# A decoder block on one core: GLU by row blocks, convolution in wide sums, merge products with tokens on the partition

## The chip, the cores and the metric

The kernel runs on one core of a Trainium2 chip. The metric is the device time of the execution in microseconds (us). Its engines are named as in the profile: PE is TensorE (matmul), PEld its weight load, DVE VectorE, ACT ScalarE, POOL GpSimd, SP SyncE, on whose queue nearly all loads are issued. Each engine works through its own instructions in the order in which the program has them.

## The reference, cut to what matters

One decoder layer over 256 tokens and 2048 channels, all in float32:

```
h    = rmsnorm(x) * (1 + sc1) + sh1          # sh1, sc1, g1, ... = silu(c) @ w_ada + b_ada
proj = h @ w_in                              # q, six k/v parts, gates, GLU input (a, g), merge gates (ga, gb)
o    = sparse attention of 16 heads
u    = causal_dwconv(a * sigmoid(g), 31 taps)
y_b  = silu(layernorm(u)) @ conv_pw_w + conv_pw_b
y_a  = o @ w_o_nsa
merged = sigmoid(ga) * y_a + sigmoid(gb) * y_b
x = x + g1 * (merged @ w_out)
x = x + g2 * conv_ffn(rmsnorm(x) * (1 + sc2) + sh2);  return rmsnorm(x)
```

The weights are some 400 MB in all, and each is read once.

## The kernel before, in words

**Products.** A weight tile of 128 x 1024 floats is loaded (`raw`, four buffers), then split: ScalarE rounds it to `hi` (L213), VectorE makes `lo = raw - hi` (L214), three buffers each; in the middle part every fourth tile takes a buffer of its own from the pool `more`. An activation is split in the same way. A product is the sum of three matmuls, hi x hi, hi x lo, lo x hi. `prod_w` (L240) holds the weights still and streams 256 tokens: its result has channels on the partition, and one row block (128 rows) of 512 columns is 12 matmuls of 256 columns (L248, L250, L251). `prod_x` (L227) holds the tokens still and streams the weights: its result has tokens on the partition, and the same row block is 6 matmuls of 512 columns (L235 to L237).

**Order.** The main line of products is emitted in program order. Beside it stand three queues: `heads_q` (attention), `conv_q` (convolution, LayerNorm) and `ada_q` (products with w_ada). After each weight tile `tick` (L117) pops those items whose engines, by the planner's account `load`, are not ahead of TensorE's. The account adds a cost per tile (L207 to L224) and one per item; an engine may lag TensorE by 8000 ns at most. `drain` empties a queue. The weight splits and the heads have high priority in the ordering of instructions on each engine.

**First stage.** w_ada's columns for sh1 and sc1 (33.5 MB) are multiplied on TensorE by groups of two column blocks (`ada_group`, L370, L379), turned into columns (L386), and give two blocks of the normed input h1 each. Beside them, for each of h1's 16 row blocks as it becomes ready, the GLU's first seven column blocks of both halves are summed in PSUM (`glu_first`, L402, L409 to L411). The other nine blocks follow as full products of 384 columns.

**Convolution.** Two blocks at a time, 30 taps of each as one multiply-add on VectorE (L457), first tap and last copy on ScalarE. Its order is that of `conv_q`, from the end of the first stage on.

**Attention.** Head by head, scores two heads ahead of values (`AHEAD`), paced by the planner's account; the products for q, the first three `ga` gates and attention share one stretch.

**Merge.** Four chunks each of ga, `w_o_nsa`, gb, `conv_pw_w`, all by `prod_w`; `merged` has channels on the partition, which is what `w_out` (by `prod_x`) needs as its stationary side. The bias of conv_pw is a column per block. Steps of ada for g1, sh2 and sc2, 96 in all, each a load of 512 KB and a multiply-add of 1024 columns on VectorE (L280), are paced by `PACE` until attention is over and by 1500 after the w_o_nsa products.

Of the kernel before, what the change touches and what calls it, by code (L numbers as in the profile page):

```python
# [16 lines left out]
P = 128  # L17
D = 2048
# [33 lines left out]
DF = 1.0  # L52
WEND = 25
TL = 1
HP = 300
AHEAD = 2
SB = 8
PACE = 5000
# [3 lines left out]
def block_kernel(ctx, tc, x, c, w_ada, b_ada, norm1_g, w_in, cmp_pe, w_kc1, w_kc2, w_vc1, w_vc2,  # L62
# [44 lines left out]
    queues = [deque(), deque(), deque()]  # L107
    heads_q, conv_q, ada_q = queues
    load = {"pe": 0.0, "dve": 0.0, "act": 0.0, "dma": 0.0}

    los = deque(maxlen=LAG)

# [4 lines left out]
    def tick():  # L117
        for e in ("dve", "act", "dma"):
            load[e] = max(load[e], load["pe"] / DF - 8000.0)
        go = True  # L120
        while go:
            go = False
            for q in queues:
                if q and all(load[e] * DF <= load["pe"] for e in q[0][0]):
                    cost, f = q.popleft()
                    use(**cost)
                    with ExitStack() as es:
                        es.enter_context(tc.issue_after(los[0]))
                        if q is heads_q and HP:
                            es.enter_context(tc.high_priority(HP))  # L130
                        f()
                    go = True

# [67 lines left out]
    ext, turn = [None], [0]  # L201

    def wtile(src, k0, nk, c0, w):
        raw = wp.tile([P, WT], F32, tag="raw", name=nm("raw"), bufs=4)
        turn[0] += 1
        pool, bufs = (ext[0], 1) if ext[0] is not None and turn[0] % 4 == 0 else (wp, 3)
        hi = pool.tile([P, WT], F32R, tag="hi", name=nm("hi"), bufs=bufs)  # L207
        lo = pool.tile([P, WT], F32R, tag="lo", name=nm("lo"), bufs=bufs)
# [9 lines left out]
    def tiles(src, nk, c0, w):  # L218
        step = WT // w
        for k0 in range(0, nk, step):  # L220
            m = min(step, nk - k0)
# [3 lines left out]
            use(pe=m * w * 2.53)  # L225
            tick()
# [13 lines left out]
    def prod_w(act, src, c0, w, nk=KB):  # L240

        nb = w // P
        acc = ps_acc.tile([P, 4, T], F32, tag="acc", name=nm("accw"))
        for k, hi, lo in tiles(src, nk, c0, w):
            for b in range(nb):
                s = slice(b * P, (b + 1) * P)
                last = k == nk - 1 and (b % 2 == 1 or b == nb - 1)
                nc.tensor.matmul(acc[:, b, :], hi[:, s], act[:, k, 0, :], start=k == 0 and b % 2 == 0, stop=False,  # L248
                                 skip_group_check=True)
                nc.tensor.matmul(acc[:, b, :], hi[:, s], act[:, k, 1, :], start=False, stop=False, skip_group_check=True)  # L250
                nc.tensor.matmul(acc[:, b, :], lo[:, s], act[:, k, 0, :], start=False, stop=last, skip_group_check=True)  # L251
        return acc[:, :nb, :]
# [90 lines left out]
    par_first()  # L343
    ss = st(NT * 2)
    for t in range(NT):
        for j in range(2):
            scr = t4([P, WT])
            nc.scalar.activation(scr, xt[:, t, j * WT:(j + 1) * WT], AF.Square, accum_out=ss[:, 2 * t + j:2 * t + j + 1])
    s2 = st(NT)
    nc.vector.reduce_sum(s2, ss.rearrange("p (t n) -> p t n", n=2), axis=AX.X)  # L350
    r = rsqrt_cols(s2, NT, 1.0 / D)
    xh = bigt([P, NT, D])
    for t in range(NT):
        nc.vector.tensor_scalar(xh[:, t, :], xt[:, t, :], r[:, t:t + 1], None, op0=ALU.mult)
    xhT = bigt([P, KB, T])
    for k in range(0, KB, 2):
        p_ = pt([P, 2, T])
        for j in range(2):
            for t in range(NT):
                nc.tensor.transpose(p_[:, j, t * P:(t + 1) * P], xh[:, t, (k + j) * P:(k + j + 1) * P], ident)  # L360
        nc.scalar.copy(xhT[:, k:k + 2, :], p_)

    h1 = actt()
    NA = 7
    u = bigt([P, KB, T])
    ada_v = w_ada[:, :2 * D].rearrange("(k p) (s c) -> p k s c", p=P, s=2)

    def ada_group(j):  # L370

        p_ = pt([P, 2, T])
        for n in range(8):
            side, k = n // 4, n % 4 * 4
            own = n % 3 == 2
            raw = (wp if own else first).tile([P, 4, T], F32, tag="araw", name=nm("araw"), bufs=2 if own else 4)
            nc.sync.dma_start(raw, ada_v[:, k:k + 4, side, j * T:(j + 1) * T])
            for i in range(4):
                nc.tensor.matmul(p_[32 * i:32 * i + 32, side, :], cz[:, k + i, :], raw[:, i, :], start=k == 0,  # L379
                                 stop=k == KB - 4, skip_group_check=True)  # L380
            yield
        acc = t4([P, 2, T])
        nc.scalar.copy(acc, p_)
        p_ = pt([P, 4])
        for i in range(4):
            nc.tensor.matmul(p_[:, i:i + 1], acc[:, i // 2, (i % 2) * P:(i % 2 + 1) * P], ones[:, 0:1], start=True, stop=True)  # L386
# [4 lines left out]
        yield  # L391

    acc_g = ps_acc.tile([P, 4, T], F32, tag="acc", name="acc_g")
    acc_a = ps_acc.tile([P, 4, T], F32, tag="acc", name="acc_a")
    acc_x = [pt([P, 2, T]) for _ in range(3)]

    def first_out(which, b):
        if b < 4:
            return (acc_g, acc_a)[which][:, b, :], b % 2
        if b < 6:  # L400
            return acc_x[which][:, b - 4, :], b - 4
        return acc_x[2][:, which, :], which  # L402
# [10 lines left out]
    with tc.tile_pool(name="first", bufs=4) as first:  # L413
# [13 lines left out]
        for _ in stream:  # L427
            pass
# [575 lines left out]
```

## Time and profile before

| | |
|---|---|
| median of 3 runs | 1765.85 us (1764.63 to 1767.06) |
| profiled execution, its own time | 1765.94 us |
| its span, first to last instruction | 1764.2 us |
| mean granted TensorE clock | 0.986 of full speed |
| read from memory | 402.8 MB, 230 GB/s over the span |

Busy times and shares are of the span. A matmul's busy time includes its way through the pipeline, so matmuls overlap: the rate of a stage is read from how far apart they start, or from their count in a window. The stages by the last instruction that reads a product: GLU to 282 us, k, v and the first half of q to 415, attention with the rest of q and three ga gates to 600, w_o_nsa and the last gate to 717, gb to 813, conv_pw to 912, w_out to 1003, then the feed-forward part, which the change does not touch.

### The profile page before, as it was taken

The numbers are of one execution on the slowest core, as the hardware profiler recorded it, in microseconds if no ns is written. First come the engines' busy times: TensorE is split into PE (matmuls) and PEld (weight loads), VectorE is DVE, ScalarE is ACT, GpSimd is POOL, SyncE is SP. The second block draws the span as 40 slices with busy tenths as digits, with TensorE's granted clock in tenths as the row PEclk, the third lists the DMA queues.
The fourth block names the chain that finished last, engine by engine and source line by source line (L and its number), as shares of the span: only waits on it lengthen the run. The fifth ranks groups of instructions, "written<-read, shape, count | busy, mean of one in ns | idle before, by whom it ended". The sixth has DMA issues, their size and how long they took to land.

```text
span 1764.2 us, 29690 instructions
## 1 busy us (share of the span) xinstructions
PE 1712.7 (97%) x11844; PEld 1551.8 (88%) x11844; DVE 1286.4 (73%) x1852; ACT 872.9 (49%) x1223; POOL 5.5 (0%) x22
## 2 busy tenths in 40 slices
PE   5999999999999999999999899999999999999997
PEld 3777999899999999999988888888888888888886
DVE  2233999998999898877886677776467776586665
ACT  4333444344768634563344465554455554345553
POOL 0000000000000000000000000000000000000000
PEclk8999999999999999999999999999999999999999
DMA  9996777884764676789887667676666767656663
GB/s 305 352 345 225 228 225 231 266 286 143 235 198 130 203 241 214 250 300 317 292 306 259 199 202 226 215 224 222 219 213 212 220 213 219 212 183 189 188 192 127
DMA packets 270198, 406.83 MB, mean 231 GB/s; under 512 B 12876, under 2 KB 181612, under 8 KB 269420
## 3 DMA queue, kind: packets, MB, share of 16 engines
q1 hardware_dynamic: 268652, 400.49, 71.4%
q10 hardware_dynamic: 1408, 4.46, 0.7%
q8 instruction: 92, 1.51, 0.4%
q14 instruction: 46, 0.38, 0.1%
HBM read 402.80 MB, written 2.10 MB: 230 GB/s over the span
## 4 chain that ended last, share of the span: by engine, by line
PE 93%; DMA 3%; DVE 2%; ACT 1%; issue 1%; SPq 0%; DVEq 0%; ACTq 0%
PE accp L261 18%; PE accw L251 11%; PE accw L248 11%; PE accw L250 11%; PE accp L262 9%; PE accx L236 6%; PE accx L237 6%; PE accx L235 6%; DMA araw<-in_w_ada_dram 2%; PE pt L379 1%; PE pt L675 1%; DVE lo L214 1%; PE pt L714 1%; PE pt L409 1%; PE pt L410 1%; PE pt L411 1%
## 5 line engine op out<-in xcount | busy, mean ns | idle before, releaser
L213 ACT CAST hi<-raw 128x1024 fp32r<-128x1024 f32 (+2 forms) x562 | 575.1, 1024 | 765.9 <-PE accw L250 273.3
L214 DVE TENSOR_TENSOR lo<-raw,hi 128x1024 fp32r<-128x1024 f32 (+2 forms) x562 | 668.6, 1191 | 375.4 <-ACT hi L213 363.8
L261 PE MATMUL accp<-act,hi 128*128 128x512 f32 x1408 | 492.4, 395 | 0.0
L251 PE MATMUL accw<-act,lo 128*128 128x256 f32 x1696 | 484.1, 286 | 2.0 <-DVE lo L214 2.0
L250 PE MATMUL accw<-act,hi 128*128 128x256 f32 x1696 | 483.8, 285 | 0.0
L248 PE MATMUL accw<-act,hi 128*128 128x256 f32 x1696 | 483.8, 285 | 0.0
L262 PE MATMUL accp<-act,lo 128*128 128x256 f32 x1408 | 393.6, 280 | 0.0
L251 PEld LDWEIGHTS accw<-act,lo 128*128 128x128 f32 x1696 | 325.5, 192 | 5.0 <-DVE lo L214 3.0
L248 PEld LDWEIGHTS accw<-act,hi 128*128 128x128 f32 x1696 | 325.8, 192 | 3.2 <-issue 2.4
L250 PEld LDWEIGHTS accw<-act,hi 128*128 128x128 f32 x1696 | 325.7, 192 | 2.4 <-issue 2.2
L261 PEld LDWEIGHTS accp<-act,hi 128*128 128x128 f32 x1408 | 264.1, 188 | 62.1 <-issue 0.2
L262 PEld LDWEIGHTS accp<-act,lo 128*128 128x128 f32 x1408 | 265.6, 189 | 0.3 <-issue 0.2
L236 PE MATMUL accx<-lo,act 128*128 128x512 f32 (+2 forms) x664 | 227.6, 343 | 1.3 <-DVE lo L214 1.3
L235 PE MATMUL accx<-hi,act 128*128 128x512 f32 (+2 forms) x664 | 227.2, 342 | 0.0
L237 PE MATMUL accx<-hi,act 128*128 128x512 f32 (+2 forms) x664 | 226.8, 342 | 0.0
L457 DVE SCALAR_TENSOR_TENSOR cacc<-big,cw,cacc 128x255 f32<-128x255 f32 (+24 forms) x480 | 201.3, 464 | 0.3
L280 DVE SCALAR_TENSOR_TENSOR t<-araw,cs,t 128x1024 f32<-128x1024 f32 x120 | 153.6, 1280 | 25.3 <-DMA araw<-in_w_ada_dram 25.2
L236 PEld LDWEIGHTS accx<-lo,act 128*128 128x128 f32 x664 | 125.8, 189 | 18.4 <-DVE lo L214 2.6
L235 PEld LDWEIGHTS accx<-hi,act 128*128 128x128 f32 x664 | 125.8, 189 | 14.5 <-ACT hi L213 0.2
L237 PEld LDWEIGHTS accx<-hi,act 128*128 128x128 f32 x664 | 125.8, 189 | 14.3 <-issue 0.4
L918 DVE SCALAR_TENSOR_TENSOR t<-t,fw,t 128x254 f32<-128x254 f32 (+1 forms) x176 | 73.5, 478 | 0.0
L916 ACT ACTIVATE t<-t,fw 128x256 f32<-128x256 f32 x88 | 48.0, 593 | 1.3 <-DVE t L913 1.3
(214 smaller groups left out, 1198.7 us busy)
## 6 DMA issues: line engine op xcount, KB each, us to landing
araw<-in_w_ada_dram SPq DMA_DIRECT2D x192, 512.0 KB, 5.4
raw<-in_ffn_w_up_dram SPq DMA_DIRECT2D x176, 512.0 KB, 4.5
raw<-in_w_in_dram SPq DMA_DIRECT2D x116, 512.0 KB, 4.6
raw<-in_ffn_w_down_dram SPq DMA_DIRECT2D x88, 512.0 KB, 4.7
raw<-in_w_in_dram SPq DMA_DIRECT2D x48, 384.0 KB, 3.9
raw<-in_w_o_nsa_dram SPq DMA_DIRECT2D x32, 512.0 KB, 4.7
raw<-in_conv_pw_w_dram SPq DMA_DIRECT2D x32, 512.0 KB, 5.5
raw<-in_w_out_dram SPq DMA_DIRECT2D x32, 512.0 KB, 4.7
```

The source lines that it names most:

```text
L213: nc.scalar.copy(hi[:, :n], raw[:, :n])
L214: los.append(nc.vector.tensor_tensor(lo[:, :n], raw[:, :n], hi[:, :n], op=ALU.subtract).ins)
L235: nc.tensor.matmul(o, act[:, k, 0, s], hi, start=k == 0, stop=False)
L236: nc.tensor.matmul(o, act[:, k, 0, s], lo, start=False, stop=False)
L237: nc.tensor.matmul(o, act[:, k, 1, s], hi, start=False, stop=k == nk - 1)
L248: nc.tensor.matmul(acc[:, b, :], hi[:, s], act[:, k, 0, :], start=k == 0 and b % 2 == 0, stop=False, skip_group_check=True)
L250: nc.tensor.matmul(acc[:, b, :], hi[:, s], act[:, k, 1, :], start=False, stop=False, skip_group_check=True)
L251: nc.tensor.matmul(acc[:, b, :], lo[:, s], act[:, k, 0, :], start=False, stop=last, skip_group_check=True)
L261: nc.tensor.matmul(acc[:, b], hi[:, s], act[:, k], start=k == 0, stop=False, skip_group_check=True)
L262: nc.tensor.matmul(acc[:, b, 0, :], lo[:, s], act[:, k, 0, :], start=False, stop=k == KB - 1, skip_group_check=True)
L280: nc.vector.scalar_tensor_tensor(acc, raw, cs[:, k:k + 1], acc, op0=ALU.mult, op1=ALU.add)
L457: nc.vector.scalar_tensor_tensor(acc[:, s:], u[:, b, :T - s], cw[:, CW - 1 - s, b:b + 1], acc[:, s:], op0=ALU.mult, op1=ALU.add)
```

## The change

- **GLU.** The 16 row blocks are worked in four quarters. For each quarter all eight chunks of 512 columns are summed over four row blocks and added into `u` and `gl` in SBUF (`glu_out`); sigmoid and product follow in the last quarter. The ada columns that a quarter of h1 needs are loaded beside the quarter before: sh1 on TensorE (`ada_pe`), sc1 on VectorE (`ada_dve`); the first two pairs (`ada_lead`) wholly on TensorE. Three quarters stand in the first stage; the last is the start of the middle part.
- **Convolution.** Three blocks at a time (six groups, the last of one block). 18 of 30 taps are a product per block on ScalarE and one sum over the group on VectorE, 12 stay as they were. One accumulator tile and one product tile. The pool `more` is gone.
- **Attention.** `AHEAD` 1; `deal(n)` spreads the queued steps evenly over the next n weight tiles.
- **Merge.** ga, w_o_nsa, gb and conv_pw by `prod_x`; `merged` has tokens on the partition and is turned for `w_out` by 32 transposes, three and four tiles behind each chunk; the bias is loaded as rows.
- **Planner.** Other costs (2.75 for 2.53 a column, 150 for 60 of VectorE a tile), `PACE` 6500; the 32 steps for g1 are queued when the taps are done, at 1500, the others get 1500 after the gb products.

```diff
+    def deal(n):
+        share[:] = len(heads_q) / n, 0.0
...
+        share[1] += share[0]
+        while heads_q and share[1] >= 1.0:
+            share[1] -= 1.0
+            give(heads_q)
...
-        pool, bufs = (ext[0], 1) if ext[0] is not None and turn[0] % 4 == 0 else (wp, 3)
...
-        use(dma=1.43 * n, act=190 + n / 1.2, dve=60 + n / 0.96)
+        use(dma=1.43 * n, act=190 + n / 1.2, dve=150 + n / 0.96)
...
+    def glu_out(q, n, acc):
+        s = slice(4 * (n // 2), 4 * (n // 2) + 4)
+        dst = (gl, u)[n % 2]
+        if q == 0:
+            nc.scalar.copy(dst[:, s, :], acc)
+            return
+        nc.vector.tensor_add(dst[:, s, :], dst[:, s, :], acc)
...
+        def ada_dve(box, q, side):
+            for k in range(0, KB, 2):
+                raw = ada_raw([P, 2, QW])
+                nc.sync.dma_start(raw, ada_v[:, k:k + 2, side, q * QW:(q + 1) * QW])
...
+            stream = ada_quarter(q + 1)
+            for n in range(8):
...
+                    acc = acc_w()
+                    sum_w(acc, h1, w_in, glu_c0(n), q * KQ, KQ, True, True)
+                glu_out(q, n, acc)
+                for _ in range(3):
+                    next(stream, None)
...
+    WIDE = tuple(s for s in range(2, CW) if s % 5 not in (0, 2)) + (1,)
...
+                nc.scalar.mul(box["p"][:, b - b0, s:], u[:, b, :T - s], cw[:, CW - 1 - s, b:b + 1])
...
+                    nc.vector.tensor_add(acc[:, :, s:], acc[:, :, s:], prod[:, :, s:])
...
+        for s in WIDE:
+            conv_q.extend(({"act": 500}, product(b, s)) for b in blk)
+            conv_q.extend(narrow.popleft() for _ in range(min(n, len(narrow))))
+            conv_q.append(({"dve": 170 + n * 265}, wide(s)))
...
-        yp = prod_w(oT, w_o_nsa, n * 512, 512)
+        yp = prod_x(oT, w_o_nsa, n * 512, 512)
...
+        yp = prod_x(uT, conv_pw_w, n * 512, 512)
+        y = t4([P, NT, 512])
+        for t in range(NT):
+            nc.vector.tensor_add(y[:, t, :], yp[:, t, :], bias)
+            nc.vector.tensor_mul(y[:, t, :], y[:, t, :], gbs[:, t, s])
+            nc.vector.tensor_add(merged[:, t, s], merged[:, t, s], y[:, t, :])
+        coming.extend([3 + i, turn_m(4 * n + 2 * i)] for i in range(2))
```

## Rows read from the trace of the kernel before

**Rows 1.** The page, part 1: busy us, share of the span, instructions.

```profile
PE 1712.7 (97%) x11844; PEld 1551.8 (88%) x11844; DVE 1286.4 (73%) x1852; ACT 872.9 (49%) x1223; POOL 5.5 (0%) x22
```

**Rows 2.** The page, part 4: the chain that ended last, by engine.

```profile
PE 93%; DMA 3%; DVE 2%; ACT 1%; issue 1%; SPq 0%; DVEq 0%; ACTq 0%
```

**Rows 3.** Windows: length, busy us (count) of each engine, clock, DMA share, GB/s.

```profile
34.00:178.00 144.00, 133.01 (x1183) 106.99 (x1180) 42.18 (x62) 47.40 (x63) 1.06 (x2) 0.93 0.92 303
178.00:282.00 104.00, 104.00 (x867) 103.84 (x866) 97.82 (x164) 46.67 (x61) 0.00 (x0) 1.00 0.80 230
282.00:415.00 133.00, 133.00 (x1128) 124.73 (x1127) 122.56 (x227) 57.15 (x69) 1.27 (x3) 1.00 0.81 255
415.00:625.00 210.00, 210.00 (x1564) 198.70 (x1563) 189.81 (x397) 139.33 (x315) 0.52 (x1) 0.98 0.59 181
836.00:912.00 76.00, 74.87 (x602) 72.83 (x601) 64.25 (x72) 28.80 (x31) 0.00 (x0) 1.00 0.87 297
912.00:1004.00 92.00, 89.30 (x489) 76.99 (x487) 60.49 (x69) 41.23 (x53) 0.00 (x0) 1.00 0.74 241
...
420.00:440.00 20.00, 20.00 (x125) 18.35 (x126) 15.10 (x43) 7.33 (x20) 0.00 (x0) 0.86 0.26 79
180.00:700.00 520.00, 520.00 (x4163) 500.27 (x4163) 477.00 (x884) 273.02 (x473) 1.79 (x4) 0.99 0.71 218
```

**Rows 4.** Timeline of PE, start and length: eleven and thirteen matmuls, first and last.

```profile
640.00 0.28 PE L251 MATMUL accw<-act,lo 128*128 128x256 f32 x1
...
641.20 0.28 PE L248 MATMUL accw<-act,hi 128*128 128x256 f32 x1
...
1500.07 0.39 PE L237 MATMUL accx<-hi,act 128*128 128x512 f32 x1
...
1502.79 0.39 PE L237 MATMUL accx<-hi,act 128*128 128x512 f32 x1
```

**Rows 5.** Timeline of PE: the first GLU matmul, the first behind the stage.

```profile
34.15 0.58 PE L409 MATMUL acc_g<-act,hi 128*128 128x256 f32 x1
...
177.92 0.28 PE L248 MATMUL accw<-act,hi 128*128 128x256 f32 x1
```

**Rows 6.** Windows of PE and PEld alone, lines 379, 386 and 155 in turn.

```profile
34.00:178.00 144.00, 32.85 (x444) 11.14 (x440) 0.93 0.92 303
...
34.00:178.00 144.00, 7.21 (x56) 6.79 (x56) 0.93 0.92 303
...
34.00:178.00 144.00, 2.79 (x10) 1.43 (x10) 0.93 0.92 303
```

**Rows 7.** Windows, as rows 3, of two stretches in which loads are dense.

```profile
60.00:140.00 80.00, 75.34 (x711) 60.30 (x710) 24.83 (x35) 26.94 (x35) 0.00 (x0) 0.98 1.04 343
780.00:800.00 20.00, 20.00 (x169) 20.00 (x169) 15.12 (x13) 8.26 (x8) 0.00 (x0) 1.00 0.97 345
```

**Rows 8.** Groups by line and shape: count, busy us, mean ns, idle before.

```profile
L214 DVE TENSOR_TENSOR lo<-raw,hi 128x1024 fp32r<-128x1024 f32 x476 | 581.9, 1223 | 286.0 <-ACT hi L213 283.0 <-PE accw L251 0.6
L684 DVE SCALAR_TENSOR_TENSOR s<-dist,pt 128x512 f32<-128x512 f32 x16 | 10.9, 683 | 0.1
...
L704 ACT ACTIVATE s<-s,st 128x256 f32<-128x256 f32 x32 | 14.3, 497 | 0.0
```

**Rows 9.** The chain in order of time: start, us, four transposes between products.

```profile
1014.07 0.44 PE pt L901 x4
```

**Rows 10.** Windows of VectorE alone, line 457 (the taps).

```profile
180.00:690.00 510.00, 201.33 (x480) 0.99 0.71 218
```

**Rows 11.** Timeline of ACT: the last gb gate is read.

```profile
813.37 1.02 ACT L840 ACTIVATE big<-accw 128x1024 f32<-128x1024 f32 x1
```

**Rows 12.** Windows of VectorE alone, line 280 (ada steps).

```profile
836.00:912.00 76.00, 23.78 (x20) 1.00 0.87 297
```

**Rows 13.** Waits: us in total, times, longest us.

```profile
DVE lo L214 <- ACT hi L213: 363.8, 315, 7.2
...
PEld accw L251 <- DVE lo L214: 3.0, 5, 1.1
```

More of the change, by code (lines that the diff above doesn't have):

```diff
@@ L122, in tick, with give @@
             go = False
[L123 to L131, printed above, removed]
-                    go = True
+            for q in (conv_q, ada_q):
+                if q and all(load[e] <= load["pe"] for e in q[0][0]):
+                    give(q)
+                    go = True
+    def give(q):
+        cost, f = q.popleft()
+        use(**cost)
+        with ExitStack() as es:
+            es.enter_context(tc.issue_after(los[0]))
+            if q is heads_q:
+                es.enter_context(tc.high_priority(HP))
+            f()
     def drain(q):
@@ L416, in block_kernel, with ada_raw @@
         nc.vector.tensor_copy(cz[:, :, 0], cs)
[L418 to L428 removed]
+        seen = [0]
+        def ada_raw(shape):
+            seen[0] += 1
+            own = seen[0] % 3 == 0
+            return (wp if own else first).tile(shape, F32, tag="araw", name=nm("araw"), bufs=2 if own else 4)
@@ new lines, in ada_quarter @@
+        def ada_quarter(q):
+            box = {}
+            js = range(q * KQ // 2, (q + 1) * KQ // 2)
+            turns = [ada_dve(box, q, 1), (x for j in js for x in ada_pe(box, j, 0))]
+            for _ in range(8):
+                for g in turns:
+                    next(g)
+                    yield
+            for g in turns:
+                for _ in g:
+                    pass
+            for n, j in enumerate(js):
+                modulate(j, halves(box[0, j]) + halves(box[1][:, n * T:(n + 1) * T]))
+                yield
@@ new lines, in ada_lead @@
+        def ada_lead(j):
+            box = {}
+            for side in range(2):
+                yield from ada_pe(box, j, side)
+            modulate(j, halves(box[0, j]) + halves(box[1, j]))
+            yield
+        par_first()
+        lead = ada_lead(0)
+        for _ in range(4):
+            next(lead)
+        ss = st(NT * 2)
+        for t in range(NT):
+            for j in range(2):
+                scr = t4([P, WT])
+                nc.scalar.activation(scr, xt[:, t, j * WT:(j + 1) * WT], AF.Square,
+                                     accum_out=ss[:, 2 * t + j:2 * t + j + 1])
@@ L486, in block_kernel @@
+    for n in range(8):
+        acc = acc_w()
+        sum_w(acc, h1, w_in, glu_c0(n), (NQ - 1) * KQ, KQ, True, True)
+        glu_out(NQ - 1, n, acc)
+        there = 2 * n + 2 if n % 2 else 0
+        while done + 3 <= there:
+            conv_blocks(done, 3)
+            done += 3
+    conv_blocks(done, KB - done)
     kcv = sgt([P, 4, T])
```

316 lines of the change are left out of this document (170 added, 146 removed).

## Prediction

> **What bounds the kernel now.** I read the busy shares first: TensorE is busy 97% of the span, VectorE 73%, ScalarE 49% [rows 1]. The chain of waits agrees: 93% of what ended last is TensorE's own work [rows 2]. A busy TensorE is not yet one at its best rate, so I then took the windows by stage and counted matmuls. In the stages from 178 us on it issues without a break: 867 instructions in 104 us, 1128 in 133 us [rows 3]. The timeline gives the rate: ten 256-column weight products take from 640.00 to 641.20 us, 0.120 us each; twelve of 512 columns from 1500.07 to 1502.79 us, 0.2267 us each [rows 4]. Only two places leave time on the table: the first stage (busy counts 133 of 144 us, but with a clock of 0.93 and, below, only 122 us of work) and the merge products with the ada loads beside them (602 instructions in 76 us, where 0.120 us would give 633) [rows 3]. VectorE is nearly full from 178 to 625 us (97.8 of 104, 122.6 of 133, 189.8 of 210 us), so it is the engine that can take a gain back; ScalarE has room in all stages [rows 3].
>
> **Term 1, GLU by row blocks.** The first product starts at 34.15 us and the first stage ends at 177.92 us [rows 5]: 143.8 us. In it TensorE does 672 GLU matmuls (7 column blocks x 2 x 3 x 16) at 0.120 = 80.6 us, ada matmuls 32.9 us, column turns of ada 7.2 us, parameter transposes 2.8 us [rows 6]; sum 123.5, so 20 us are lost there. Then the other 9 blocks, 864 matmuls at 0.120 = 103.7 us, end the GLU at 281.6 us. After the change three quarters of the GLU run beside the loads: 1152 matmuls = 138.2 us. Half of the ada columns go from TensorE to VectorE, which leaves 320 of 512 ada instructions, some 256 of them after 34 us, at 32.85/444 each = 18.9 us; turns and transposes stay at 10. Sum 167 us, ending at 201 us without a gap; the last quarter adds 384 x 0.120 = 46.1, to 247 us. What could hold it: the transfers (w_ada 33.5 MB, three quarters of the GLU weights 25.2 MB, x 2.1 MB: 61 MB at the 343 GB/s of the loaded stretch [rows 7] are 178 us, less than 201), and VectorE (48 splits at 1.22 = 59, 48 ada sums of 512 columns by the nearest row, 0.68, = 33, 16 sums of GLU blocks at 1.22 = 20, some 10 more [rows 8]: 122 of 167 us; it had 42 of 144 [rows 3]). So TensorE becomes the bound of this stage, but three engines at 75 to 100% with queues in order won't run without gaps: I take 10 us lost, half of today's, end at 257 us, gain 25 us. Ends: 34 (no gap), 13 (today's 20 us stay).
>
> **Term 2, merge products.** Sixteen products of 512 columns and 16 row blocks change from weights-stationary to tokens-stationary. A row block costs 12 x 0.120 = 1.440 us now and 6 x 0.2267 = 1.360 us after [rows 4]; 256 row blocks x 0.080 = 20.5 us gained, all on the path. Added: merged must be turned back, 32 transposes at 0.44/4 = 0.11 us [rows 9], 3.5 us. Net 17.
>
> By the Trainium skill (TensorE: Matmul & The Clock Gate, Back-to-back issue gap) an isolated matmul is followed after N/2.4 + 2.5 ns, 109 ns for 256 columns and 216 for 512. By that rule the swap would gain only 4 us instead of 20.5; the trace does not agree for 256 columns (120 ns [rows 4]).
>
> **Term 3, the convolution.** 480 taps cost 201.3 us of VectorE [rows 10], 0.419 each. 288 of them become a ScalarE product and a wide sum: 120.7 us leave VectorE; 90 sums of three blocks (about 720 columns, between 0.68 for 512 and 1.22 for 1024 [rows 8]: 0.90) and 18 of one (0.42) add 88.6. VectorE gains 32 us; ScalarE gets 288 x 0.49 (the scaled 256-column ACTIVATE, 497 ns [rows 8]) = 141 us. None of this is on the path by itself. But the conv starts after the last GLU quarter's second pair (about 217 us, now 180) and has a shorter span to finish in, so VectorE stays as full as it was. All 480 taps are done by 690 us now [rows 10] and conv_pw starts when the last gate has been read at 813 us [rows 11], so some 50 us of delay are covered. I put this at 0; ends -4 (VectorE is relieved) and +6.
>
> **Term 4, attention.** 415 to 625 us holds six products (138 us) and 72 us of attention; ScalarE is busy 139 us, VectorE 190 us of 210 [rows 3]. About a third of the new ScalarE products falls here (38 sums, 114 products x 0.49 = 56 us), so ScalarE goes to some 195 of 205 us with exponentials and transposed copies in TensorE's chain. Spreading the heads evenly and looking one head ahead instead of two evens the peaks but lets a head's chain show. I take +4 us; ends -6 (the clock dip to 0.86 from 420 to 440 us goes [rows 3]) and +20.
>
> **Term 5, ada beside the merge products.** The planner gives ada loads less before conv is done (pace 6500 for 5000) and puts them behind it. A tile of a product allows 2816 - 1464 = 1352 ns of other transfers, so 0.9 of a step of 1500; VectorE's account allows (2816 - 1217 - 700)/1130 = 0.8, plus what is unspent. In the four conv_pw products that is some 30 steps instead of the 20 of 836 to 912 us [rows 12]. VectorE then needs 32 x 1.22 + 30 x 1.28 + merges of 5.5 us each (six 512-column operations of 0.68, two splits of 0.69) = 99 us in 91; the transfers are 62 x 0.524 MB = 32.5 MB, 94 us at 345 GB/s [rows 7]. The stage already loses 4 us at 20 steps, and waits for lo are what it loses them to [rows 13]. I take +8; ends 0 (the backlog slides into the w_out products, where VectorE has 60 of 92 us [rows 3]) and +13. No further ada work is left at the end of w_out, so the drain behind it costs nothing. The sum merged needs 4.1 us of VectorE behind the last conv_pw product; its transposes are held back three and four tiles (8 and 11 us), which covers it, unless VectorE is behind by more than 4 us; that is within the +13. The bias rows travel on ScalarE's queue, four of 256 KB, hidden.
>
> **Sum.** -25 - 20.5 + 3.5 + 0 + 4 + 8 = -30 us. The profiled execution took 1765.9 us (span 1764.2 and 1.7 around it), the median of the runs is 1765.85, so both give **1736 us**.
>
> **Rivals.**
> 1. Everything hides: the first stage runs without gaps (-34), ada slides into w_out (0), attention gains 4: 1765.9 - 34 - 17 - 4 = 1711 us. For it: VectorE loses 32 us of taps, and 60 of 92 us in w_out. Against: the 4 us already lost at 20 steps.
> 2. Little is left: the gaps of the first stage stay (-13), the merge stage costs its full 13, attention 8: 1765.9 - 13 - 17 + 13 + 8 = 1757 us. For it: three nearly full engines in order.
> 3. Slower: the wide sum waits for ScalarE. There is one product tile, so each sum frees it, three products follow, and the next sum stands on VectorE in front of later weight splits. ScalarE's queue holds its weight copies, which wait for TensorE (lo waited for hi 363.8 us in 315 waits, 1.15 us each [rows 13]). If VectorE is blocked 0.8 us at each of 108 sums, that is 86 us; it has about 43 free in this part (520 us from 180 to 700 less 477 busy [rows 3]; after the change the span is shorter by some 45 us, and its work, by the taps and the GLU splits done earlier, by as much), so 43 come through: 1779 us. It decides from (43 + 30)/108 = 0.68 us a sum. Against: the twelve plain taps of each block stand between the products, 0.42 us each, and three buffers of hi and lo give TensorE 5.8 us of lead.
> 4. The page's spacing: term 2 gains 4 less 3.5, the rest as forecast: 1753 us.
>
> **Chances.** Forecast 0.52 (its own range 1724 to 1748), rival 1 0.20, rival 2 0.14, rival 3 0.11, rival 4 0.03. A change of 0.2% (3.5 us) is what a measurement of this kernel can tell. Faster: 0.52 + 0.20 + 0.03 and 0.09 of rival 2 = 0.84; the same 0.05, the upper end of rival 2; slower 0.11, rival 3. Eight in ten lie from 1708 to 1764: rival 1 with 3 us of room, and rival 2 with a stall of 7 us more; left out is rival 3.
>
> **What would show it.** The GLU's last matmul near 257 us, and a granted clock nearer 1 than 0.93 in the first stage; 90 matmuls of 512 columns in 20 us in all merge products; stalls behind lo in conv_pw of 8 us; ScalarE above 90% in attention. The forecast is wrong if the GLU ends after 270 us, or if VectorE sits idle before the wide sums for over half a microsecond each.

## The result, and the profile after: slower by 0.7%

The changed kernel takes 1778.57 us (median of 4, 1777.32 to 1779.70) against 1765.24 us for the kernel before: ratio 1.0071, 95% interval 1.0051 to 1.0091. The forecast was 1736 us. Busy shares and the chain of waits of the kernel after, which answer to [rows 1, 2]:

```profile
PE 1690.7 (95%) x10148; PEld 1467.6 (83%) x10148; DVE 1322.6 (74%) x1732; ACT 982.3 (55%) x1489; POOL 6.1 (0%) x28
...
PE 83%; DVE 6%; DMA 5%; ACT 4%; issue 2%; DVEq 0%; SPq 0%; ACTq 0%
```

TensorE has 22 us less to do, as intended, but a tenth of the chain has gone from it to VectorE, ScalarE and the loads. The place is found by following the same events through both kernels. In the timeline of the kernel after (start, length, line): the compressed keys are read, the third ga gate, the last exponential of the last head, the first and the second w_o product, the reciprocals of the LayerNorm's variance, the last gb gate, the second w_out product.

```profile
285.29 1.01 ACT L595 COPY sg<-accw 128x1024 f32<-128x1024 f32 x1
540.07 1.00 ACT L839 COPY sg<-accx 128x1024 f32<-128x1024 f32 x1
615.88 0.19 ACT L796 ACTIVATION_READ_ACCUMULATOR s<-s,st 128x1 f32 x1
633.88 1.22 DVE L947 TENSOR_TENSOR big<-accx,sg 128x1024 f32<-128x1024 f32 x1
642.84 1.22 DVE L947 TENSOR_TENSOR big<-accx,sg 128x1024 f32<-128x1024 f32 x1
771.77 1.75 DVE L907 RECIPROCAL t<-t 128x256 f32<-128x256 f32 x1
804.60 1.02 ACT L953 ACTIVATE big<-accx 128x1024 f32<-128x1024 f32 x1
969.44 1.28 DVE L1004 TENSOR_TENSOR t<-accx,gb 128x512 f32<-128x512 f32 x2
```

The same events in the kernel before (the last gb gate is [rows 11]):

```profile
305.87 1.01 ACT L488 COPY sg<-accw 128x1024 f32<-128x1024 f32 x1
596.46 1.02 ACT L731 COPY sg<-accw 128x1024 f32<-128x1024 f32 x1
594.37 0.19 ACT L688 ACTIVATION_READ_ACCUMULATOR s<-s,st 128x1 f32 x1
624.98 1.22 DVE L831 TENSOR_TENSOR big<-accw,sg 128x1024 f32<-128x1024 f32 x1
648.33 1.22 DVE L831 TENSOR_TENSOR big<-accw,sg 128x1024 f32<-128x1024 f32 x1
732.62 1.75 DVE L791 RECIPROCAL t<-t 128x256 f32<-128x256 f32 x1
957.89 1.29 DVE L874 TENSOR_TENSOR t<-accx,gb 128x512 f32<-128x512 f32 x2 [0.41 <-PE accx L237]
```

The differences give the account. An event marks TensorE's progress only where TensorE hasn't run ahead of it. When the first w_o product of the kernel after is read, some 59 of the second one's 96 matmuls are done (37 are left, from 634 to 643 us), and when its last conv_pw product is read, at 931 us, 60 of w_out's are done, so these two events are no ends of a stretch here; the second w_o product and the second w_out product are. The forecast column splits the terms of the prediction over the same stretches (a merge product at 16 x 0.080 = 1.28 us; five lie in the second stretch, seven in the third, four in the fourth).

| stretch | forecast | measured |
|---|---|---|
| start to the compressed keys | -25 | -20.6 |
| to the second w_o product | -6.4 + 4 = -2.4 | +15.1 |
| to the last gb gate | -9.0 | -3.3 |
| to the second w_out product | -5.1 + 3.5 + 8 = +6.4 | +20.3 |
| to the end of the span | 0 | 0.0 |
| span of the profiled execution | -30 | +11.5 |

So the first stage's gain came, and two stretches gave it back and more: of the 41.5 us between forecast and result, 17.5 lie in the second stretch and 13.9 in the fourth, 5.7 in the third and 4.4 in the first. Windows of the kernel after (length, busy us and count of PE, PEld, DVE, ACT, POOL, clock, DMA share, GB/s), to be read against [rows 3]: the first stage, the stretch between third gate and first w_o product, and conv_pw.

```profile
34.00:201.00 167.00, 159.68 (x1374) 144.50 (x1366) 106.75 (x132) 64.80 (x77) 0.00 (x0) 0.96 0.94 312
...
540.00:634.00 94.00, 78.22 (x372) 60.52 (x371) 74.26 (x152) 73.59 (x194) 0.63 (x2) 0.95 0.33 110
...
805.00:931.00 126.00, 111.61 (x483) 90.23 (x484) 103.59 (x102) 43.54 (x45) 0.00 (x0) 0.93 0.91 322
```

From 540 to 634 us TensorE runs the w_o products head by head as the heads come (156 of the 372 instructions); the others are mostly the heads' small ones. It is idle for 15.8 of the 94 us, and the loads fall to 110 GB/s. The kernel before has no wait of TensorE from 415 to 650 us. The waits of TensorE and the loads' hold on VectorE from 400 to 1020 us (total, times, longest) name the rest:

```profile
DVE t L299 <- DMA araw<-in_w_ada_dram: 21.2, 23, 2.5
...
PE pt L312 <- DVE t L299: 11.4, 1, 11.4
...
PE accx L248 <- DVE lo L226: 10.5, 8, 5.0
...
PE pt L764 <- DVE t L758: 8.0, 1, 8.0
...
PE pt L817 <- ACT s L812: 5.4, 2, 4.5
```

L764 and L817 are in the attention; 7.9 of the 10.5 us of waits for lo come by 812 us, behind the LayerNorm's work on VectorE; L312 turns an ada column at 917 us and waits for the sums of ada steps (L299), which wait for their tiles. VectorE's timeline shows what the wait at L764 was for. L748 and L758 are steps of a softmax of the attention, L548 and L567 the taps and wide sums of the convolution:

```profile
556.14 1.23 DVE L226 TENSOR_TENSOR lo<-raw,hi 128x1024 fp32r<-128x1024 f32 x1
557.28 1.19 DVE L548 SCALAR_TENSOR_TENSOR cacc<-big,cw,cacc 128x229 f32<-128x229 f32 x3
559.01 0.40 DVE L748 TENSOR_REDUCE st<-t 128x16 f32<-128x240 f32 x1 [0.55 <-ACT t L742]
559.33 0.89 DVE L567 TENSOR_TENSOR cacc<-cacc,cprod 128x711 f32<-128x711 f32 x1
...
561.71 0.89 DVE L567 TENSOR_TENSOR cacc<-cacc,cprod 128x705 f32<-128x705 f32 x1
562.52 0.41 DVE L758 TENSOR_TENSOR t<-t,st 128x240 f32<-128x240 f32 x1
```

From 554.6 to 563.0 us, while TensorE waits, taps and sums take some 5 us of VectorE.

### The profile page after: what moved, and what is told of

It is laid out like the page before. It is cut to its first block, busy times and chain, and to the rows that moved or that the text cites. A ratio compares the mean times of both kernels' runs of the same rounds, so it can differ in the third digit from the quotient of the medians.

```text
span 1775.7 us, 26510 instructions
## 1 busy us (share of the span) xinstructions
PE 1690.7 (95%) x10148; PEld 1467.6 (83%) x10148; DVE 1322.6 (74%) x1732; ACT 982.3 (55%) x1489; POOL 6.1 (0%) x28
## 4 chain that ended last, share of the span: by engine, by line
PE 83%; DVE 6%; DMA 5%; ACT 4%; issue 2%; DVEq 0%; SPq 0%; ACTq 0%
PE accp L280 18%; PE accx L248 11%; PE accx L249 10%; PE accx L247 10%; PE accp L281 9%; PE accw L259 6%; PE accw L262 6%; PE accw L261 6%; DMA araw<-in_w_ada_dram 4%; DVE t L299 2%; DVE lo L226 2%; PE pt L420 1%; ACT cprod L558 1%; ACT hi L225 1%; ACT s L796 1%
## 5 line engine op out<-in xcount | busy, mean ns | idle before, releaser
L225 ACT CAST hi<-raw 128x1024 fp32r<-128x1024 f32 x546 | 572.4, 1049 | 684.0 <-PE accx L249 287.7
L226 DVE TENSOR_TENSOR lo<-raw,hi 128x1024 fp32r<-128x1024 f32 x546 | 665.3, 1220 | 315.8 <-ACT hi L225 313.9
L280 PE MATMUL accp<-act,hi 128*128 128x512 f32 x1408 | 492.3, 395 | 0.0
L248 PE MATMUL accx<-lo,act 128*128 128x512 f32 (+2 forms) x1176 | 433.3, 369 | 10.9 <-DVE lo L226 10.5
L247 PE MATMUL accx<-hi,act 128*128 128x512 f32 (+2 forms) x1176 | 430.6, 367 | 1.8 <-ACT act L348 1.4
L249 PE MATMUL accx<-hi,act 128*128 128x512 f32 (+2 forms) x1176 | 430.9, 367 | 0.0
L280 PEld LDWEIGHTS accp<-act,hi 128*128 128x128 f32 x1408 | 264.1, 188 | 61.9
L259 PE MATMUL accw<-act,hi 128*128 128x256 f32 x896 | 258.6, 289 | 3.3 <-ACT act L348 3.3
L262 PE MATMUL accw<-act,lo 128*128 128x256 f32 x896 | 256.2, 286 | 0.0
L261 PE MATMUL accw<-act,hi 128*128 128x256 f32 x896 | 256.1, 286 | 0.0
L247 PEld LDWEIGHTS accx<-hi,act 128*128 128x128 f32 x1176 | 223.0, 190 | 38.7 <-ACT act L348 2.2
L249 PEld LDWEIGHTS accx<-hi,act 128*128 128x128 f32 x1176 | 223.1, 190 | 35.6 <-issue 2.1
L259 PEld LDWEIGHTS accw<-act,hi 128*128 128x128 f32 x896 | 173.6, 194 | 10.7 <-issue 6.8
L262 PEld LDWEIGHTS accw<-act,lo 128*128 128x128 f32 x896 | 173.5, 194 | 2.9 <-issue 2.1
L261 PEld LDWEIGHTS accw<-act,hi 128*128 128x128 f32 x896 | 173.7, 194 | 1.7 <-issue 1.5
L299 DVE SCALAR_TENSOR_TENSOR t<-araw,cs,t 128x1024 f32<-128x1024 f32 x120 | 153.6, 1280 | 22.9 <-DMA araw<-in_w_ada_dram 22.6
L558 ACT ACTIVATE cprod<-big,cw 128x253 f32<-128x253 f32 (+17 forms) x288 | 123.4, 488 | 22.0 <-DVE cacc L567 19.0
L567 DVE TENSOR_TENSOR cacc<-cacc,cprod 128x759 f32<-128x759 f32 (+24 forms) x102 | 83.7, 821 | 8.8 <-ACT cprod L558 7.5
L548 DVE SCALAR_TENSOR_TENSOR cacc<-big,cw,cacc 128x254 f32<-128x254 f32 (+8 forms) x192 | 80.7, 461 | 1.4 <-ACT cacc L541 0.9
```

The lines of the kernel that those rows point to most:

```text
L225: nc.scalar.copy(hi[:, :n], raw[:, :n])
L226: los.append(nc.vector.tensor_tensor(lo[:, :n], raw[:, :n], hi[:, :n], op=ALU.subtract).ins)
L247: nc.tensor.matmul(o, act[:, k, 0, s], hi, start=k == 0, stop=False)
L248: nc.tensor.matmul(o, act[:, k, 0, s], lo, start=False, stop=False)
L249: nc.tensor.matmul(o, act[:, k, 1, s], hi, start=False, stop=k == nk - 1)
L280: nc.tensor.matmul(acc[:, b], hi[:, s], act[:, k], start=k == 0, stop=False, skip_group_check=True)
```

## The experiments

All were timed in 3 rounds beside the kernel before. The table has, for each run, the median, the ratio to the kernel before, and from its timeline the us at which the third ga gate, the last exponential, the first and the second w_o product, the LayerNorm's reciprocals, the last gb gate and the second w_out product are reached.

| run | us | ratio (95%) | gate 3 | last exp | w_o 1 | w_o 2 | LN | gb 4 | w_out 2 |
|---|---|---|---|---|---|---|---|---|---|
| before | 1765.24 | | 596 | 594 | 625 | 648 | 733 | 813 | 958 |
| after | 1778.57 | 1.0071 (1.0051-1.0091) | 540 | 616 | 634 | 643 | 772 | 805 | 969 |
| conv_undone | 1787.08 | 1.0112 (1.0083-1.0140) | 541 | 622 | 642 | 650 | 772 | 813 | 976 |
| even_undone | 1778.28 | 1.0064 (1.0040-1.0087) | 552 | 621 | 640 | 649 | 805 | 807 | 968 |
| pace4000 | 1799.60 | 1.0184 (1.0158-1.0210) | 546 | 621 | 643 | 650 | 822 | 804 | 990 |
| all_three | 1790.62 | 1.0136 (1.0109-1.0164) | 548 | 605 | 628 | 636 | 802 | 789 | 975 |
| glu_undone | 1781.58 | 1.0085 (1.0059-1.0111) | 567 | 628 | 651 | 661 | 687 | 829 | 971 |
| b_glu | 1805.30 | 1.0210 (1.0189-1.0231) | 553 | 592 | 611 | 627 | 840 | 791 | 994 |
| b_merge | 1767.04 | 1.0005 (0.9991-1.0020) | 585 | 616 | 643 | 655 | 745 | 816 | 961 |
| half_taps | 1751.18 | 0.9918 (0.9887-0.9949) | 548 | 595 | 621 | 626 | 643 | 795 | 939 |
| b_half_taps | 1766.65 | 1.0002 (0.9989-1.0015) | 602 | 575 | 626 | 649 | 645 | 816 | 954 |
| half_ada | 1762.76 | 0.9979 (0.9965-0.9993) | 544 | 626 | 645 | 651 | 783 | 821 | 955 |
| b_half_ada | 1767.93 | 1.0003 (0.9992-1.0014) | 599 | 608 | 633 | 656 | 727 | 826 | 961 |
| b_merge_half_ada | 1759.86 | 0.9949 (0.9929-0.9968) | 587 | 615 | 638 | 651 | 731 | 819 | 952 |
| deal_fast | 1782.10 | 1.0096 (1.0081-1.0112) | 541 | 621 | 639 | 645 | 774 | 807 | 970 |
| deal_faster | 1781.25 | 1.0090 (1.0069-1.0110) | 550 | 617 | 639 | 645 | 774 | 808 | 972 |
| glu_deal_fast | 1778.55 | 1.0075 (1.0060-1.0090) | 563 | 630 | 650 | 661 | 681 | 828 | 969 |
| glu_hold | 1783.69 | 1.0101 (1.0064-1.0139) | 587 | 612 | 632 | 644 | 814 | 804 | 970 |
| after_hold | 1852.06 | 1.0487 (1.0451-1.0523) | 571 | 586 | 605 | 624 | 819 | 776 | 1039 |
| glu_hold_fast | 1783.34 | 1.0096 (1.0080-1.0113) | 576 | 627 | 646 | 656 | 773 | 823 | 976 |

### One part undone

conv_undone: all taps on VectorE again.

```
-        for s in WIDE:
-            conv_q.extend(({"act": 500}, product(b, s)) for b in blk)
...
+        conv_q.extend(({"dve": 390}, tap(b, s)) for s in range(1, CW) for b in blk)
```

> The changed kernel with all 30 taps of each block as multiply-adds on VectorE again (three blocks at a time), none on ScalarE; all else as changed. Theory 1 (the convolution's ScalarE products fill ScalarE during attention, the heads fall behind the products that should hide them, and TensorE idles behind the last ga product): the idle time between 540 and 600 us goes, the first w_o_nsa product ends some 20 us earlier (614 instead of 634), total 1758 to 1768, a part of the gain being lost again to VectorE's 32 us of taps. Theory 2 (spreading the heads and looking one head ahead is what exposes a head's chain): the idle time stays within 5 us, total 1778 to 1790.

It is some 8 us slower than the kernel after (the two intervals touch), and the last exponential is no earlier. The ScalarE products did not make the attention late; the lighter sums are rather a gain.

even_undone: heads issued by the planner's account again, still one ahead.

```
-        share[1] += share[0]
-        while heads_q and share[1] >= 1.0:
...
-            for q in (conv_q, ada_q):
+            for q in (heads_q, conv_q, ada_q):
```

> The changed kernel with the heads popped by the planner's account again instead of evenly (still one head ahead of the values); all else as changed. Theory 2: the idle time behind the last ga product goes, total 1755 to 1765. Theory 1: the same ScalarE work in the same stretch, idle time moved but not gone, total 1773 to 1785.

The median is that of the kernel after. The last exponential comes at 621 for 616 us, the LayerNorm 33 us later, and the ada wait ahead of w_out is less: three changes that cancel. The dealing alone is not what made it slow.

pace4000: PACE = 4000 for 6500. all_three: this, conv_undone, and heads by the account two ahead.

> The changed kernel with ada steps at pace 4000 instead of 6500 before the convolution is done, so that some 20 more of the 96 steps are over before the conv_pw products. Theory 3 (the ada steps put behind the convolution make loads and VectorE the bound of the conv_pw and w_out products, and a column turn of ada stops TensorE for 11 us): that stall goes and the stretch from the last gb gate to the end of w_out shortens by 15 to 20 us, total 1758 to 1765. Rival (the merge sums on VectorE are what is late): within 5 us of 1778.

> The GLU by row blocks and the tokens-stationary merge products alone: convolution on VectorE, heads by the planner's account and two ahead, ada steps at pace 4000. If theories 1 to 3 name the whole loss: 1735 to 1745, as the gains of the first stage (21 us) and of the merge products (17 us) then come through. If the merge products themselves lose time in a way not named yet: 1755 or more.

pace4000 lies above both of its expectations: ada steps that come earlier push the LayerNorm back by 50 us (822), and the end by 21. With all three undone the first w_o product and the last gb gate come early (628, 789), but the LayerNorm's reciprocals come at 802, TensorE waits 22 us for its results, and the kernel is 12 us slower than after. What one queue gives up, another loses: a first sign, no more, that VectorE's total decides.

glu_undone: the first stage and GLU of the kernel before put into the kernel after, the blocks of u going to the convolution three at a time as they come.

> The kernel after with the first stage and the GLU of the kernel before (seven blocks of u whole at 180 us, the rest by three); wide convolution sums, even attention, merge products and pace 6500 stay. Theory (with row blocks no u block is whole before the last quarter, so the convolution starts some 40 us later and VectorE's queue decides the middle): the LayerNorm starts before 670 us instead of 711, conv_pw starts by 815, median 1740 to 1757, so at least 20 us under the kernel after and under the kernel before too. Rival (the row blocks' 21 us count, and the loss lies in the loads of the ada steps): KC comes at 306 instead of 285, the median stays within 8 us of the kernel after, 1771 to 1790.

Half of this came true: the LayerNorm's reciprocals come at 687 instead of 772 us. But the median did not move. The GLU ends 20 us later, and from the compressed keys to the second w_o product it takes 355 us against 358 in the kernel after, so the convolution's early start does not help the heads; from there to the second w_out product the 16 us are won that make up for most of it.

### One part alone, on the kernel before

b_glu: GLU by row blocks alone. b_merge: the tokens-stationary merge products with their transposes alone.

```
-        yp = prod_w(oT, w_o_nsa, n * 512, 512)
+        yp = prod_x(oT, w_o_nsa, n * 512, 512)
```

> The kernel before with the GLU by row blocks alone. Theory 4 (the convolution, fed later, and the LayerNorm behind it decide when conv_pw can start, so what TensorE gains in front of them is lost waiting for them): GLU ends 20 us earlier, total within 8 us of before (1759 to 1772). Theory 5 (the row blocks are a plain gain and the loss of the change is made by the other parts): 1742 to 1750.

> The kernel before with tokens-stationary merge products alone, transposes three and four tiles behind. Both theories: TensorE has 17 us less to do; LayerNorm was done some 28 us before conv_pw needed it, and twelve products in front of conv_pw get 15 us shorter, so it still is in time: 1749 to 1756. If the shorter products run into VectorE or the loads instead: 1760 or more.

b_glu shows the price of row blocks by themselves: the compressed keys are read at 286.28 us (20 us earlier), the second w_o product is 21 us earlier, so the gain comes through the attention whole, and the kernel is 40 us slower, far outside both expectations. TensorE's waits from 780 to 860 us in b_glu (total, times, longest) are the LayerNorm (L820, L336 and L337 are its sums and the split of its output):

```profile
PE pt L835 <- DVE t L820: 30.1, 1, 30.1
PE pt L853 <- DVE t L820: 15.7, 1, 15.7
PE accw L247 <- ACT act L336: 8.2, 1, 8.2
```

In b_merge it takes 271 us from the first w_o to the last conv_pw product instead of 288. Windows, b_merge first, then the kernel before:

```profile
643.00:914.00 271.00, 264.55 (x1160) 214.47 (x1160) 234.35 (x261) 126.79 (x135) 0.00 (x0) 0.99 0.83 285
625.00:913.00 288.00, 285.96 (x2341) 282.49 (x2340) 243.12 (x277) 132.94 (x144) 0.00 (x0) 1.00 0.82 274
```

But 12 of these 17 us are a head start: in b_merge half of the second w_o product is done when the first is read. From the second w_o to the second w_out product b_merge takes 305.4 us instead of 309.6, 4 us less where 11 were forecast. A product that nothing disturbs does gain what was forecast: in after_hold the third and the fourth gb gate are read 21.8 us apart, in the kernel before 23.0. The second w_o product comes 7 us later, the first 18. The third gate is done 12 us earlier, the heads 22 us later. VectorE's timeline of b_merge in the heads' tail shows what stands in its queue: an ada sum waiting for its tile, weight splits and taps, and between them the last heads' small steps (L335).

```profile
623.26 2.62 DVE L285 SCALAR_TENSOR_TENSOR t<-araw,cs,t 128x1024 f32<-128x1024 f32 x2 [2.76 <-DMA araw<-in_w_ada_dram]
625.80 1.22 DVE L219 TENSOR_TENSOR lo<-raw,hi 128x1024 fp32r<-128x1024 f32 x1
626.93 0.82 DVE L462 SCALAR_TENSOR_TENSOR cacc<-big,cw,cacc 128x227 f32<-128x227 f32 x2
627.66 0.42 DVE L335 TENSOR_TENSOR act<-pt,act 128x256 fp32r<-128x256 f32 x1
```

### Work taken away

half_taps leaves out 15 of the convolution's 30 taps of the kernel after, b_half_taps as many of the kernel before.

```
-    WIDE = tuple(s for s in range(2, CW) if s % 5 not in (0, 2)) + (1,)
+    WIDE = tuple(s for s in range(2, 16) if s % 5 not in (0, 2)) + (1,)
```

> The changed kernel with 15 of 30 taps of each block left out (9 of 18 wide sums and 6 of 12 plain taps), so the output is not the reference's: some 90 us less for VectorE and 65 us less for ScalarE before the LayerNorm. Theory 4: the heads and the LayerNorm come earlier, idle time behind the last ga product and at the gb products goes, total 1735 to 1755. Theory 5 (something else, such as the ada loads, makes the loss): 1768 to 1780.

> The kernel before with 15 of the convolution's 30 taps left out (so its convolution is not the reference's). It is the control for half_taps, where the same cut took 27 us from the kernel after. Theory (in the kernel before VectorE's convolution still ends in time, and conv_pw finds its input ready): within 10 us of the kernel before, 1755 to 1766. Rival (VectorE work in this stretch costs TensorE time whatever the order, because the weight splits stand in the same queue): 20 to 30 us faster here too, 1735 to 1747.

The same cut is worth 27 us in the kernel after and nothing in the kernel before, though it brings the last exponential forward in both (616 to 595, 594 to 575). In the kernel before TensorE never waits for the heads, so their coming earlier wins nothing; in the kernel after it is idle for 15.8 us behind the third gate, and in half_taps, over about the same work, for 2.8:

```profile
540.00:622.00 82.00, 79.18 (x369) 61.80 (x368) 52.11 (x93) 59.17 (x145) 0.00 (x0) 1.00 0.33 115
```

half_ada, b_half_ada and b_merge_half_ada leave out 48 of the 96 ada steps ahead of w_out: 25 MB of loads and 48 sums of 1.28 us, no TensorE matmul of a product.

```
-        return [({"dve": 1130, "dma": pace}, step(k)) for k in range(KB)]
+        return [({"dve": 1130, "dma": pace}, step(k)) for k in range(n)]
```

> The changed kernel with half of the row blocks left out of the ada sums for g1, sh2 and sc2 (48 steps of 512 KB instead of 96), so the output is not the reference's. Theory 3 again, by taking the cost away instead of moving it: the 11 us stall and the slow w_out go, total 1752 to 1762. If only the conv and LayerNorm matter: 1770 or more.

> The kernel before with 48 of the 96 deferred ada steps left out (so its modulations are not the reference's): 25 MB less to load and 48 fewer VectorE sums of 1.1 us, no TensorE work less. Control for the next run. PE is busy 98 us of every 100 between 720 and 920 us in the kernel before, so little can be won: 1755 to 1765.

> The kernel before with the tokens-stationary merge products and with the same 48 ada steps left out. Theory (the merge products' 17 us were lost in b_merge because weights and ada tiles together keep the DMA queues at 0.85 to 0.91 of their time from 720 to 920 us, so that a shorter product waits for its next tile): with fewer loads the gain appears, 10 to 17 us under b_half_ada, about 1740 to 1752. Rival (VectorE's added work per product, or the attention's end that sets the first merge product, swallows it): within 5 us of b_half_ada.

16 us in the kernel after, none in the kernel before, 7 in b_merge. The 11 us wait at 917 us is gone in half_ada, and from the last gb gate to the second w_out product it takes 133.5 us instead of 164.8; but its last gb gate comes 17 us later, so the 16 us are a net figure. b_merge_half_ada falls between its two expectations: the ada steps, loads and sums together, take about 7 of b_merge's missing 17 us; that the late heads take the rest is not shown.

### The order of the attention

deal_fast: deal(24), deal(12), deal(15) for deal(32), deal(18), deal(23). deal_faster: 16, 8, 10. glu_deal_fast: deal_fast on glu_undone.

> The kernel after with the attention's steps dealt over 24, 12 and 15 weight tiles instead of 32, 18 and 23. Theory (the even dealing stretches the attention): the first head's softmax comes by 424 us instead of 432, the last by 600 instead of 616, the first w_o product ends by 618 instead of 634, median 1757 to 1771. Rival (VectorE and ScalarE set the pace of the heads, with the convolution's taps and products in the same queues): the last softmax stays at 608 or later, PE waits for heads inside the products instead of behind them, median 1773 to 1786.

> The same with 16, 8 and 10 weight tiles. Theory: earlier still, last softmax by 590 us, first w_o product by 610, median 1750 to 1768. Rival: as before, 1773 to 1790, or slower still, since PE stands in line behind heads that aren't ready.

> The kernel after with the old first stage and GLU, as in glu_undone (1781.6 us), and the attention dealt over 24, 12 and 15 tiles. Theory: the attention is all that glu_undone lost (first w_o product at 651 us against 625 in the kernel before; from there to the end it was 13 us quicker than the kernel before), so the first w_o product ends by 632 and the median is 1755 to 1766. Rival: within 6 us of glu_undone.

My theory that the even dealing stretches the attention fell: apart from the third gate, no event moves by more than 6 us.

glu_hold: on glu_undone, no convolution step is issued while steps of heads are queued. after_hold: the same on the kernel after. glu_hold_fast: glu_hold with the dealing of deal_fast.

```
             for q in (conv_q, ada_q):
+                if q is conv_q and hold[0] and heads_q:
+                    continue
```

> glu_undone (the kernel after with the old first stage, 1781.6 us), and no step of the convolution is issued while steps of the heads are queued. Theory (VectorE's queue decides: in glu_undone 63 us of taps stood between the heads from 432 to 620 us, and the LayerNorm was over at 687 us, 140 us before conv_pw could begin): the last softmax comes by 595 instead of 628, the first w_o product ends by 620 instead of 651, the LayerNorm is over by 790, median 1740 to 1762, faster than both kernels. Rival (the heads are a chain of their own, whatever stands between them): first w_o product at 640 or later, 1772 to 1790.

> The kernel after (row blocks) with the same hold. Theory: the heads end by 590 and the first w_o product by 605 instead of 634, but the 55 us of taps held back come after it, so that the LayerNorm starts 20 to 40 us later than 711 and conv_pw waits for it: 1775 to 1800, no faster than the kernel after, because VectorE's work up to the LayerNorm is the bound there and not its order. Rival (order is all): 1745 to 1765.

> glu_hold (1783.7 us) with the attention dealt over 24, 12 and 15 weight tiles. Theory (VectorE's queue decides; with no taps between the heads the dealing sets their pace, and the taps are let go some 25 us sooner): last softmax by 595 us instead of 612, first w_o product by 617 instead of 632, LayerNorm over by 795 instead of 814, conv_pw waits under 12 us, median 1748 to 1768. Rival (the heads' own chain is at its floor in glu_hold): first w_o product at 628 or later, 1772 to 1788.

The hold moves the heads as the theory says: first w_o product 19 us earlier in glu_hold, 29 in after_hold. It also moves the LayerNorm as far back as it must: 814 and 819 us, where conv_pw could have begun at 804 and 776. TensorE's waits in after_hold from 770 to 830 us:

```profile
PE pt L889 <- DVE t L874: 29.8, 1, 29.8
PE accx L250 <- ACT act L351: 10.7, 1, 10.7
PE pt L907 <- DVE t L874: 10.3, 1, 10.3
```

The times I gave were wrong all the same: in glu_hold the last exponential came 17 us later than expected and the LayerNorm 24 us later, and after_hold lost three times what I allowed. That loss lies behind conv_pw, whose last product is read at 921 us, 10 us sooner than in the kernel after: the steps for g1 are queued when the taps are done, so 35 ada sums fall between 920 and 1040 us where the kernel after has 19, and TensorE waits 29 us for one of them at 988 us and 14 us for lo. In glu_hold_fast the heads' queue is emptied sooner, taps are let go sooner, and the heads end at 627 again. No version here beats the kernel before by rearranging; only leaving work out did.

## Why the prediction was wrong

The steps that failed are three: Term 4's "+4 us" for the attention, Term 5's "+8" for the ada steps beside the merge products, and under both of them Term 3's "None of this is on the path by itself".

**Term 1** was right in kind and 4 us too large: -20.6 for -25. The first stage runs at a clock of 0.96 instead of 0.93, TensorE busy 160 of 167 us.

**Term 2** had the right price for a product, 21.8 for 23.0 us undisturbed, and rival 4, by which nearly all of this would be missing, is out. Its sum of 17 us came in no run: b_merge shows 4 of the 11 us of its last eleven products, and the 5.7 us missing in the third stretch of the table are of this kind.

**Term 3** put the convolution at 0 because "some 50 us of delay are covered". The prediction names the end of the taps at 690 us and the start of conv_pw at 813, and not the LayerNorm between them, which is VectorE's work too. Its last split, in the kernel before, the kernel after and b_glu:

```profile
766.78 1.22 DVE L330 TENSOR_TENSOR act<-big,act 128x1024 fp32r<-128x1024 f32 x1
...
807.21 1.22 DVE L349 TENSOR_TENSOR act<-big,act 128x1024 fp32r<-128x1024 f32 x1
...
855.99 3.50 DVE L337 TENSOR_TENSOR act<-big,act 128x1024 fp32r<-128x1024 f32 x3 [3.65 <-ACT act L336]
```

So 45 us were covered, from 768 to 813 us. In the kernel after the delay uses them up (808 us, with the last gate read at 805), and it costs some 8 us of waits for lo; in b_glu, without the lighter sums, it costs 54 us of waits and the kernel 40. What Term 3 did not price at all is the queue: the taps stand on VectorE between the steps of the heads, and half of them are worth 27 us in the kernel after against 0 in the kernel before (half_taps and its control). It is not that the later start put more of them there. VectorE's work on the accumulator (`cacc`) from 432 to 620 us, the kernel before, then after:

```profile
432.00:620.00 188.00, 64.02 (x149) 1.00 0.60 187
...
432.00:620.00 188.00, 57.73 (x99) 0.97 0.47 146
```

The same taps cost nothing while TensorE has other work beside the heads, and time where it does not. The saving on VectorE was sized well, and helps:

```profile
L558 ACT ACTIVATE cprod<-big,cw 128x253 f32<-128x253 f32 (+17 forms) x288 | 123.4, 488 | 22.0 <-DVE cacc L567 19.0
L567 DVE TENSOR_TENSOR cacc<-cacc,cprod 128x759 f32<-128x759 f32 (+24 forms) x102 | 83.7, 821 | 8.8 <-ACT cprod L558 7.5
L548 DVE SCALAR_TENSOR_TENSOR cacc<-big,cw,cacc 128x254 f32<-128x254 f32 (+8 forms) x192 | 80.7, 461 | 1.4 <-ACT cacc L541 0.9
```

With the six last sums, which write `u` (L565, 5.2 us), this is 170 us for 201.3 [rows 10], 32 less, as forecast.

**Term 4** was +4, with +20 as its upper end, and measured +21.5 (15.1, and the 6.4 us that five merge products should have gained there). Its mistake is one of method: I added the cost of the heads to TensorE's time, as if TensorE would go on setting the pace. In the kernel after it is idle for 15.8 us behind the third gate, 8.0 of them for a softmax on VectorE with taps in between and 5.4 for ScalarE. It reaches that gate 56 us sooner, but only 24 us of this are gained (20.6 and three merge products); the rest is work of the heads left behind the gate, 216 instructions of TensorE that belong to no product where the kernel before has 38. A TensorE that comes early is not enough for such a loss: in b_glu it comes 20 us early, no wait in the attention is over 0.5 us, and the 20 us are kept. Neither ScalarE's products (conv_undone) nor the dealing (even_undone, deal_fast) is the reason by itself.

**Term 5** named the place, the mechanism and the direction; +8, with +13 as its upper end, should have been +22 (20.3, and the 1.6 us that the products should have gained over their transposes). VectorE's ada sums (L299, L280 in the kernel before) from 860 to 980 us, the kernel after first:

```profile
860.00:980.00 120.00, 43.61 (x34) 0.93 0.89 307
...
860.00:980.00 120.00, 25.55 (x20) 1.00 0.82 277
```

Fourteen steps more, 18 us of VectorE, in a stretch that moves 307 GB/s of the 345 that the dense one reached [rows 7]. I put the turns of the ada columns in no one's way; one stopped TensorE for 11.4 us. half_ada takes 16 us off.

**Rival 3** gave 1779 us, the time that was measured, by luck. Its sums waited for ScalarE 7.5 us in 102, 0.07 us each, where 0.68 was to decide. It was right only that VectorE's queue would be where the gain is lost. Neither of the two signs that were to show the forecast wrong came: the GLU's last product is read at 262 us, and the wide sums hardly wait.

What stays open: which part of the change leaves the heads so late. No part undone by itself removes the loss, and in all_three, which has the row blocks and the merge products alone, the second w_o product still comes 15 us later than the two gains together would put it (636 for 621 us). The merge products alone end the heads 22 us later, with no VectorE work added ahead of that. The ada tile that VectorE waits for in the tail may explain some of it (in b_merge_half_ada the second w_o product comes at 651 instead of 655 us); but with half of the ada steps gone the heads end later in both kernels (626 and 608 us), and no run here separates the causes. Nor do these runs show how early the heads could end with the best order: the earliest with all the work in was 586 us, in after_hold.

## What to carry to other kernels

When an engine is 97% busy, find out where it will meet the results of another engine if it comes sooner, and what stands in that engine's queue there: b_glu keeps its 20 us past the heads, the kernel after has 5.5 of its 20.6 left at the second w_o product. Measure a stretch between events that the busy engine can't have run ahead of; the first w_o product overstated the loss in the attention by 14 us. A piece of work that is "not due until later" has to be priced in the queue it stands in, behind each consumer of that queue, and not only at its own due time. Control the taking away of work on both kernels: the same cut worth 27 us in the kernel after and 0 in the kernel before says which of them is bound by it.

## What the runs showed of the hardware

Here a wait of TensorE cost more than its length. Windows of the kernel after, before, in and behind the wait at 917 us:

```profile
900.00:917.00 17.00, 17.00 (x84) 14.16 (x82) 14.69 (x15) 7.32 (x9) 0.00 (x0) 1.00 0.85 292
917.00:931.00 14.00, 2.57 (x12) 2.10 (x11) 8.06 (x8) 1.04 (x1) 0.00 (x0) 0.66 0.89 299
931.00:945.00 14.00, 13.87 (x51) 10.89 (x52) 12.85 (x17) 3.07 (x4) 0.00 (x0) 0.73 0.74 226
```

Behind the wait TensorE is busy for 13.9 us of 14 and issues 51 instructions; at the rate ahead of it, 84 in 17 us, it would have been 69. Eight of the 51 are short transposes, so some 4 us are lost at the least. The granted clock of 0.73 is a mixture of its two levels, 1.2 and 2.4 GHz: products of 512 columns follow each other every 0.43 us up to 938 us and every 0.23 us from 941 us on. The Trainium skill (TensorE: Matmul & The Clock Gate, Part 1: The HAM clock gate) says that the array's clock is at the lower level after it has been idle and at the higher one after it has been busy; the trace agrees, with 1.00 ahead of the wait, 0.66 in it and 0.73 behind it.
